# Scalings of the softmax on three engines, unit orders tried at build time, and norms spread by transposes

## The chip, the cores and the metric

The kernel runs on one core of one Trainium2 chip. Its engines are TensorE (PE, matrix products, with PEld for the loading of the stationary operand), VectorE (DVE), ScalarE (ACT), GpSimd (POOL) and SyncE (SP), whose queue issues every DMA here. The metric is device time of one execution in microseconds (us). All data is float32; the products run in three passes over operands that are split into a high and a low part.

## The reference, cut to what matters

512 tokens of 1024 features pass through four stages. Each begins with an RMS norm over the 1024 features of a token.

```
layer A : x + (rglru(conv(h@w_in)) * silu(gate)) @ w_out          h = rmsnorm(x, g)
layer B : x + (swa(q, k, v) * silu(gate)) @ w_out                 16 heads of 64, window 128, sinks
block 2 : x + (sig(ga)*(gqa@w_a) + sig(gb)*(nbr@w_b)) @ w_out      8 heads of each kind
MLP     : x + relu(rmsnorm(x)@w_up)**2 @ w_down, then a last rmsnorm

softmax of a head, with its sink:  p = exp(s - m) / (sum(exp(s - m)) + exp(sink - m))
rmsnorm:                           y = x * rsqrt(mean(x*x) + eps) * g
```

## The kernel before

Activations are kept transposed, features on partitions and the 512 tokens along the free axis. Each product of a 128x128 weight tile with 512 tokens is three matmuls (high x high, high x low, low x high). A weight column block of 128 outputs (a "unit", 512 KB for 1024 inputs) is brought in by a DMA from SP's queue, copied to its high part (ACT, DVE or POOL, lines 322 and 331) and subtracted to its low part (DVE, line 346).

The order of the work is not written out. Each piece is a generator that yields operations, and a planner (`Sched`) runs when the kernel is built: it keeps a clock per engine with a price for each operation, takes among the operations that could start soonest the one of the best priority, and emits it. What it emits is the order of each engine's queue on the chip, where every engine then works in order. So a change of a price, a priority or a limit moves instructions on all engines.

Three parts of it matter here.

- **Norms** (`rstd_chain`). Four matmuls with a column of ones (line 396, 128x1) sum the squares of the 512 tokens, one column of 128 tokens each; POOL raises the mean to the power -0.5 (line 386), which gives `col`, 128 partitions by 4 columns. What the later stages need is the same numbers along the free axis on all partitions (`nrm.bc`). For that DVE multiplies the identity by `col` (128x512, line 346), one product with a matrix of ones spreads it (`ps<-fb,ones`, two hardware passes), and ACT copies it out of PSUM (line 322). The norms a, b, m and f stand ahead of layer A, layer B, block 2 and the MLP.
- **Attention units** (`attn_unit`). One unit is 4 heads of one block of 128 queries (in the neighborhood attention one head of all 512). It scales the mask (layer B only, line 374), multiplies q and k (matmuls with 256 or 384 columns), takes maximum and sum of mask and scores on DVE (line 972, its own code), exponentiates on ACT, multiplies by the reciprocal of the sum (line 374, four times), transposes on TensorE (line 420), splits, and multiplies by v. Both scalings are `PMUL`, which has POOL alone. At most `MAXU` = 4 units are under way at a time. Layer B has 16 units, block 2 eight of the first kind and eight of the second.
- **Work beside the units.** While units run, TensorE is filled with the projections of the same stage (`main`, in a fixed order). In layer B the last of these is `b_w_out`, whose first products take features 0 to 5 of 8 and whose later ones need features 6 and 7, which come from the last four units.

PSUM has 8 banks; a unit holds one for each pair of score products until DVE has read them.

Of the kernel before, what the change touches and what calls it, by code (L numbers as in the profile page):

```python
# [15 lines left out]
P = 128  # L16
# [14 lines left out]
MAXU = 4  # L31
# [4 lines left out]
AVOID = 600.0  # L36
# [37 lines left out]
class Op:  # L74
# [3 lines left out]
    def __init__(self, opts, reads, writes):  # L78
# [3 lines left out]
        self.ready = None  # L82


class Task:
    def __init__(self, gen, prio):
        self.gen = gen
        self.prio = prio
        self.op = None


class Sched:
# [3 lines left out]
    def __init__(self):  # L96
# [20 lines left out]
    def spawn(self, gen, prio=3):  # L117
        t = Task(gen, prio if callable(prio) else (lambda: prio))
        self.tasks.append(t)
        return t  # L120

# [26 lines left out]
    def run(self):  # L148
        while self.tasks:
# [12 lines left out]
            for t in self.tasks:  # L162
                if isinstance(t.op, Op):
                    best = None
                    for o, rdy in zip(t.op.opts, t.op.ready):
                        c = self.clock[o[0]]
                        s = max(c, rdy)
                        f = s + o[1] + (AVOID if o[0] == "POOL" and len(t.op.opts) > 1 else 0.0)
# [23 lines left out]
            emit()  # L192
# [55 lines left out]
def kernel(ctx: ExitStack, tc: tile.TileContext, io: dict, out: bass.AP):  # L248
    nc = tc.nc
    S = Sched()  # L250
# [56 lines left out]
    def A(o, i, fn, scale=None, bias=None, accum=None, also=None):  # L307
# [30 lines left out]
        return Op(opts, rd, wr)  # L338
# [304 lines left out]
    def rstd_chain(nrm):  # L643
# [1039 lines left out]
    layer_a()  # L1683
    layer_b()
    block2()
    mlp()

    def main():
        for fn in jobs:
            yield from fn()  # L1690
# [9 lines left out]
    with tc.manual_schedule():  # L1700
# [15 lines left out]
        S.run()  # L1716
# [117 lines left out]

# [15 lines left out]
```

## Time and profile before

| what | us |
|---|---|
| median of 3 runs | 1137.48 (1136.98 to 1137.63) |
| the profiled execution | 1139.5 |
| its span, first to last instruction | 1137.7 |
| TensorE busy | 1119.6 |
| VectorE / ScalarE / GpSimd busy | 758.7 / 384.1 / 306.6 |

The profiled execution lies 2.0 us above the median, 1.8 us of its time is outside the span. A busy TensorE is not a TensorE at its peak: matmuls are pipelined, so the busy time of one overlaps that of the next, and what a matmul costs is the step from its start to the next start.

### The profile page before, as it was taken

How to read it: one execution, taken by the hardware profiler on the slowest of the kernel's cores; microseconds unless marked ns; L12 is line 12 of the kernel's file. 1: busy time of each engine (PE TensorE's matmuls, PEld its weight loads, DVE VectorE, ACT ScalarE, POOL GpSimd, SP SyncE). 2: the span in 40 equal slices, each digit the busy share in tenths (PEclk: the TensorE clock that was granted, in tenths of full speed). 3: DMA queues.
4: the chain of work that ended last, by engine and by line, in shares of the span. 5: the costliest groups of instructions: out<-in, count | busy, mean ns of one | idle time of the engine just before them, and what ended most of it. 6: DMA issues, size and time to landing. Idle time of an engine off the chain costs nothing.

```text
span 1137.7 us, 14747 instructions
## 1 busy us (share of the span) xinstructions
PE 1119.6 (98%) x5316; PEld 931.7 (82%) x5316; DVE 758.7 (67%) x1344; ACT 384.1 (34%) x781; POOL 306.6 (27%) x404
## 2 busy tenths in 40 slices
PE   8999999999999899999999999999999999999997
PEld 6788888888888688788888888888888888888887
DVE  7999998775777886568666565876554225556332
ACT  5457761234566631156444251111111111111001
POOL 1222333135586532032322224312110003113100
PEclk9999999999999899999999999999999999999998
DMA  7333445108133330820463645523233322223001
GB/s 290 87 117 107 145 141 193 56 1 257 40 96 95 134 102 12 238 102 29 134 191 111 176 133 174 185 75 111 79 117 118 112 74 89 78 93 111 1 1 74
DMA packets 46793, 127.42 MB, mean 112 GB/s; under 512 B 6272, under 2 KB 7936, under 8 KB 46720
## 3 DMA queue, kind: packets, MB, share of 16 engines
q1 hardware_dynamic: 46720, 126.47, 35.0%
q8 instruction: 42, 0.69, 0.2%
q14 instruction: 31, 0.25, 0.1%
HBM read 106.53 MB, written 2.10 MB: 95 GB/s over the span
## 4 chain that ended last, share of the span: by engine, by line
PE 93%; DVE 2%; issue 2%; DMA 1%; ACT 1%; POOL 1%; SPq 0%; POOLq 0%; DVEq 0%
PE ps L396 90%; PE ps L420 3%; DVE fb L360 1%; DMA fb<-in_mk 1%; POOL fb L374 0%; DMA fb<-in_x 0%; DVE rb L346 0%; SPq L426 0%; ACT rb L322 0%; DVE fb L346 0%; ACT fb L322 0%; DMA rb<-rb 0%; DVE fb L972 0%; DVE fb L1632 0%; POOLq L1846 0%
## 5 line engine op out<-in xcount | busy, mean ns | idle before, releaser
L396 PE MATMUL ps<-rb 128*128 128x512 f32 (+2 forms) x4856 | 1087.1, 383 | 5.1 <-DMA rb<-rb 1.6
L396 PEld LDWEIGHTS ps<-rb 128*128 128x128 f32 x4856 | 878.0, 188 | 177.6 <-issue 3.0
L331 POOL TENSOR_SCALAR rb<-fb 128x1024 fp32r<-128x1024 f32 (+5 forms) x163 | 175.5, 1087 | 564.2 <-PE ps L396 407.4
L346 DVE TENSOR_TENSOR rb<-fb,rb 128x1024 fp32r<-128x1024 f32 (+5 forms) x305 | 289.0, 972 | 40.9 <-ACT rb L322 37.1
L322 ACT ACTIVATE rb<-fb 128x512 fp32r<-128x512 f32 (+4 forms) x131 | 96.9, 745 | 307.0 <-DVE fb L360 155.4
L346 DVE TENSOR_TENSOR fb<-ps,fb 128x512 f32<-128x512 f32 (+3 forms) x142 | 83.6, 590 | 156.7 <-PE ps L396 141.0
L374 POOL TENSOR_SCALAR fb<-fb,sm 128x256 f32<-128x256 f32 (+2 forms) x128 | 74.9, 603 | 125.3 <-DVE sm L389 97.1
L346 DVE TENSOR_TENSOR fb<-fb 128x512 f32<-128x512 f32 (+1 forms) x120 | 88.9, 747 | 23.3 <-ACT rb L322 21.1
L360 DVE SCALAR_TENSOR_TENSOR fb<-ps,fb 128x512 f32<-128x512 f32 x56 | 38.5, 688 | 58.4 <-PE ps L396 58.3
L346 DVE TENSOR_TENSOR rb<-ps,rb 128x512 fp32r<-128x512 f32 (+2 forms) x86 | 52.3, 612 | 37.5 <-ACT rb L322 35.5
L322 ACT ACTIVATE fb<-fb 128x512 f32<-128x512 f32 (+1 forms) x66 | 39.4, 612 | 102.6 <-DVE fb L346 83.7
L322 ACT ACTIVATE rb<-ps 128x512 fp32r<-128x512 f32 (+2 forms) x86 | 46.0, 538 | 82.1 <-PE ps L420 73.8
L322 ACT ACTIVATE fb<-fb,sm 128x256 f32<-128x256 f32 (+2 forms) x128 | 65.2, 512 | 21.2 <-DVE sm L368 16.1
L322 ACT ACTIVATE rb<-fb,vec 128x512 fp32r<-128x512 f32 x41 | 28.4, 719 | 101.1 <-DVE fb L346 98.9
L322 ACT ACTIVATE fb<-ps 64x256 f32<-64x256 f32 (+2 forms) x68 | 30.1, 442 | 82.5 <-PE ps L396 72.4
L420 PE MATMUL ps<-ident,fb 128*128 128x128 f32 x328 | 52.3, 276 | 5.4 <-POOL fb L374 4.5
L420 PEld LDWEIGHTS ps<-ident,fb 128*128 128x128 f32 x328 | 41.3, 142 | 17.2 <-POOL fb L374 6.2
L972 DVE CUSTOM_DVE_ANT_0 fb<-ps,fb 128x256 f32<-128x256 f32 (+1 forms) x64 | 29.4, 486 | 10.8 <-DMA fb<-in_mk 5.2
L972 DVE CUSTOM_DVE_ANT_0 fb<-ps,fb,sm_qs 128x256 f32<-128x256 f32 (+1 forms) x64 | 27.0, 443 | 7.3 <-PE ps L396 4.9
L374 POOL TENSOR_SCALAR fb<-fb,sm_qt 128x256 f32<-128x256 f32 (+1 forms) x64 | 30.6, 498 | 2.2 <-DMA fb<-in_mk 2.2
L360 DVE SCALAR_TENSOR_TENSOR rb<-fb,vec,rb 128x512 fp32r<-128x512 f32 x41 | 30.5, 763 | 0.6 <-ACT rb L322 0.4
L360 DVE SCALAR_TENSOR_TENSOR fb<-fb,vec 128x512 f32<-128x512 f32 x36 | 30.2, 856 | 0.0
(84 smaller groups left out, 327.0 us busy)
## 6 DMA issues: line engine op xcount, KB each, us to landing
rb<-rb SPq DMA_DIRECT2D x128, 128.0 KB, 2.5
fb<-in_w_down SPq DMA_DIRECT2D x32, 512.0 KB, 3.7
fb<-in_w_in SPq DMA_DIRECT2D x31, 512.0 KB, 4.2
fb<-in_w_up SPq DMA_DIRECT2D x29, 512.0 KB, 3.5
fb<-in_a_w_in SPq DMA_DIRECT2D x22, 512.0 KB, 3.7
fb<-in_b_w_in SPq DMA_DIRECT2D x16, 512.0 KB, 4.7
fb<-in_mb SPq DMA_DIRECT2D x8, 640.0 KB, 5.9
fb<-in_a_w_out SPq DMA_DIRECT2D x8, 512.0 KB, 3.8
```

What stands on the lines that cost most here:

```text
L322: opts = [("ACT", dur, lambda: nc.scalar.activation(out=o, in_=i, func=fn, **kw), TABLES.get(fn))]
L331: lambda: nc.gpsimd.tensor_scalar(out=o, in0=i, scalar1=1.0, scalar2=1.0, op0=ALU.mult, op1=ALU.mult), None,
L346: lambda: nc.vector.tensor_tensor(out=o, in0=a, in1=b, op=op), None,
L360: lambda: nc.vector.scalar_tensor_tensor(out=o, in0=a, scalar=s, in1=b, op0=op0, op1=op1), None,
L374: lambda: nc.gpsimd.tensor_scalar(out=o, in0=a, scalar1=s, scalar2=1.0, op0=ALU.mult, op1=ALU.mult), None,
L396: nc.tensor.matmul(out=o, lhsT=l, rhs=r, start=st, stop=sp)
L420: nc.tensor.transpose(o, i, ident)
L972: nc.vector.tensor_tensor_reduce(out=pt[h], in0=PS[:, b, o0:o0 + nk], in1=m, scale=sc, scalar=-3.0e38, op0=ALU.add, op1=ALU.max, accum_out ...
```

## The change

`PMUL` gets three choices (POOL, ACT with 800 ns added to its end in the comparison, DVE with 1200 ns), and the penalty for POOL in the operations that could run elsewhere moves from the planner into the operation. `MAXU` goes from 4 to 6. Each task of the planner gets a random number between 0 and 1 added to its priority, drawn from a seed per stage; before the kernel is built, the planner runs through each of the four stages with 8 seeds without emitting anything, and the seed whose TensorE clock is lowest at the end of the stage is kept (seed 0 adds nothing). The numbers drawn here are 0, 1, 5 and 0 for layer A, layer B, block 2 and the MLP. In `rstd_chain` the product with the identity and the product with ones go; in their place TensorE transposes each column of `col`, repeated 128 times by its access pattern.

```diff
-MAXU = 4
+MAXU = 6
-AVOID = 600.0
+JITTER = 1.0
+ORDERS = 8
...
+    def draw(self, t):
+        t.noise = JITTER * self.rng.random() if self.rng else 0.0
+
+    def next_part(self):
+        self.part += 1
+        if self.part == len(self.seeds):
+            if self.trial:
+                raise Enough()
+            return
+        self.rng = random.Random(self.seeds[self.part]) if self.seeds[self.part] else None
+        for t in self.tasks:
+            self.draw(t)
...
-                        f = s + o[1] + (AVOID if o[0] == "POOL" and len(t.op.opts) > 1 else 0.0)
+                        f = s + o[1] + t.op.late.get(o[0], 0.0)
...
-                        score = t.prio() - max(age, 0.0) / AGE
+                        score = t.prio() + t.noise - max(age, 0.0) / AGE
...
     def PMUL(o, a, s):
-        return Op([(
-            "POOL", 262.0 + 0.832 * _free(o),
-            lambda: nc.gpsimd.tensor_scalar(
-                out=o, in0=a, scalar1=s, scalar2=1.0, op0=ALU.mult, op1=ALU.mult
-            ), None,
-        )], [a, s], [o])
+        n = _free(o)
+        return Op([
+            ("POOL", 262.0 + 0.832 * n, lambda: nc.gpsimd.tensor_scalar(
+                out=o, in0=a, scalar1=s, scalar2=1.0, op0=ALU.mult, op1=ALU.mult), None),
+            ("ACT", 286.0 + 0.833 * n, lambda: nc.scalar.activation(out=o, in_=a, func=AF.Copy, scale=s), None),
+            ("DVE", 220.0 + 0.524 * n, lambda: nc.vector.tensor_scalar(
+                out=o, in0=a, scalar1=s, scalar2=None, op0=ALU.mult), None),
+        ], [a, s], [o], {"ACT": 800.0, "DVE": 1200.0})
...
-        dg = yield from fa.get()
-        yield TT(
-            f_(dg).rearrange("p (b t) -> p b t", b=4),
-            ident.unsqueeze(1).to_broadcast([P, 4, P]),
-            col.unsqueeze(2).to_broadcast([P, 4, P]),
-            ALU.mult,
-        )
         b = yield from pa.get()
-        yield MMS([(p_(b), ones, f_(dg), True, True, 858.0)])
-        fa.free(dg)
+        yield TRS([(PS[:, b, j * P:(j + 1) * P], col[:, j:j + 1].to_broadcast([P, P])) for j in range(4)])
         yield A(f_(bc), p_(b), AF.Copy)
...
+def _orders(arrays):
+    arrays = {name[3:]: v for name, v in arrays.items()}
+    best = ()
+    for _ in range(4):
+        times = []
+        for seed in range(ORDERS):
+            try:
+                times.append((_trial(arrays, best + (seed,)), seed))
+            except AssertionError:
+                pass
+        best += (min(times)[1],)
+    return best
```

What moves, engine by engine, at three places. Of the 192 scalings that stood on POOL, 27 are now on ACT (16 of masks, 11 of exponentials) and 10 on DVE (5 and 5).

**Place 1: TensorE's queue at norm a, early in layer A.** `ones,fb` are the sums of squares, `fb,ones` the product with ones, `ident,col_a` the transposes. Before:

```order
L396 MATMUL ps<-rb 128x512 x69
L396 MATMUL ps<-ones,fb 128x1 x4
L396 MATMUL ps<-rb 128x512 x15
L396 MATMUL ps<-fb,ones 128x512
L396 MATMUL ps<-rb 128x512 x915
```

and after the change:

```order
L426 MATMUL ps<-rb 128x512 x69
L426 MATMUL ps<-ones,fb 128x1 x4
L426 MATMUL ps<-rb 128x512 x12
L450 MATMUL ps<-ident,col_a 128x128 x4
L426 MATMUL ps<-rb 128x512 x918
```

The spreading stands three matmuls earlier and is four transposes. Norms m and f move the same way; at norm b the transposes stand where the product stood.

**Place 2: TensorE's queue at the end of layer B's attention.** The first row is the last group of score products (256 columns); `ident,fb` are the transposes of probabilities, four or eight in a row, which wait for the scalings; the 512-column rows are projections and products with v. Before (followed by eight transposes, 8 matmuls, four transposes and 183 matmuls):

```order
L396 MATMUL ps<-rb 128x256 x4
L396 MATMUL ps<-rb 128x512 x3
L420 MATMUL ps<-ident,fb 128x128 x4
L396 MATMUL ps<-rb 128x512 x16
L420 MATMUL ps<-ident,fb 128x128 x4
L396 MATMUL ps<-rb 128x512 x10
L420 MATMUL ps<-ident,fb 128x128 x8
L396 MATMUL ps<-rb 128x512 x3
L420 MATMUL ps<-ident,fb 128x128 x4
L396 MATMUL ps<-rb 128x512 x10
L420 MATMUL ps<-ident,fb 128x128 x4
L396 MATMUL ps<-rb 128x512 x5
```

and after the change (followed by 8 matmuls, four transposes, 5 matmuls, four transposes and 166 matmuls):

```order
L426 MATMUL ps<-rb 128x256 x4
L450 MATMUL ps<-ident,fb 128x128 x8
L426 MATMUL ps<-rb 128x512 x35
L450 MATMUL ps<-ident,fb 128x128 x4
L426 MATMUL ps<-rb 128x512 x15
L450 MATMUL ps<-ident,fb 128x128 x4
L426 MATMUL ps<-rb 128x512 x31
L450 MATMUL ps<-ident,fb 128x128 x4
L426 MATMUL ps<-rb 128x512 x9
L450 MATMUL ps<-ident,fb 128x128 x4
L426 MATMUL ps<-rb 128x512 x8
L450 MATMUL ps<-ident,fb 128x128 x4
```

Between the last scores and the last transposes stand 55 matmuls before and 111 after. Behind the last transposes the first matmul that waits for features 6 and 7 is the 49th before and the 32nd after.

**Place 3: SP's queue where block 2's first mask (`in_mk`, 128x1536) is fetched.** `rb<-rb` are moves of q and k parts between partitions, `in_w_in` weight units. Before:

```order
L426 DMA rb<-rb 64x512 x4
L426 DMA fb<-in_w_in 128x1024
L426 DMA rb<-rb 64x512 x4
L426 DMA fb<-in_w_in 128x1024
L426 DMA fb<-in_mk 128x1536
L426 DMA rb<-rb 64x512 x4
L426 DMA fb<-in_w_in 128x1024
L426 DMA fb<-in_mk 128x1536
```

and after the change:

```order
L456 DMA rb<-rb 64x512 x4
L456 DMA fb<-in_w_in 128x1024
L456 DMA rb<-rb 64x512 x4
L456 DMA fb<-in_mk 128x1536
L456 DMA fb<-in_w_in 128x1024
L456 DMA rb<-rb 64x512 x4
L456 DMA fb<-in_mk 128x1536
```

The mask is issued ahead of one weight unit that it followed. TensorE's queue at the same place, from the first score products of block 2 on, before:

```order
L396 MATMUL ps<-rb 128x384 x4
L396 MATMUL ps<-rb 128x512 x3
L396 MATMUL ps<-rb 128x256 x8
L396 MATMUL ps<-rb 128x384 x4
L396 MATMUL ps<-rb 128x256 x4
L396 MATMUL ps<-rb 128x512 x15
L396 MATMUL ps<-rb 128x384 x4
```

and after the change:

```order
L426 MATMUL ps<-rb 128x384 x2
L426 MATMUL ps<-rb 128x256 x4
L426 MATMUL ps<-rb 128x384 x2
L426 MATMUL ps<-rb 128x256 x4
L426 MATMUL ps<-rb 128x512 x3
L426 MATMUL ps<-rb 128x384 x2
L426 MATMUL ps<-rb 128x256 x4
L426 MATMUL ps<-rb 128x384 x2
L426 MATMUL ps<-rb 128x512 x6
L426 MATMUL ps<-rb 128x384 x2
```

Seven groups of score products (two matmuls of 384 columns, or four of 256, fill a bank) now stand with 3 matmuls of 512 columns among them where 3 stood too, and the eighth comes after 6 more instead of 15.

## Rows read from the trace of the kernel before

**Rows 1.** The page: its head, and busy time (share of the span) and instructions.

```profile
span 1137.7 us, 14747 instructions
PE 1119.6 (98%) x5316; PEld 931.7 (82%) x5316; DVE 758.7 (67%) x1344; ACT 384.1 (34%) x781; POOL 306.6 (27%) x404
```

**Rows 2.** TensorE's waits: total us, times, longest us.

```profile
PE ps L420 <- POOL fb L374: 4.5, 4, 1.6
PE ps L396 <- DMA rb<-rb: 1.6, 2, 1.4
PE ps L396 <- DVE sm L972: 1.5, 1, 1.5
```

**Rows 3.** Stretches: length, busy us (instructions) by engine, clock, DMA share, GB/s.

```profile
380.00:400.00 20.00, 15.47 (x66) 11.56 (x66) 15.62 (x40) 14.06 (x43) 11.81 (x19) 0.83 0.53 184
...
460.00:480.00 20.00, 20.00 (x97) 16.88 (x95) 8.19 (x12) 3.19 (x3) 1.06 (x1) 1.00 0.99 266
...
389.00:395.00 6.00, 5.95 (x18) 4.79 (x19) 3.93 (x9) 2.39 (x7) 4.72 (x10) 0.54 0.73 246
```

**Rows 4.** The chain that ended last: start us, us, what.

```profile
251.23 0.44 PE ps L420 x4
...
688.09 413.86 PE ps L396 x1830
...
1104.34 6.47 PE ps L396 x54
```

**Rows 5.** Timeline at norms a and b: start us, us, engine, line, count.

```profile
25.25 3.71 PE L396 MATMUL ps<-rb 128*128 128x512 f32 x15
...
26.46 1.03 POOL L386 TENSOR_TENSOR col_a<-sm,half 128x4 f32<-128x4 f32 x1 [24.49 <-DVE sm L368]
...
28.90 1.13 PE L396 MATMUL ps<-fb,ones 128*128 128x512 f32 x2
...
30.06 0.60 ACT L322 ACTIVATE fb<-ps 128x512 f32<-128x512 f32 x1 [9.73 <-PE ps L396]
...
244.53 1.02 PE L396 MATMUL ps<-fb,ones 128*128 128x512 f32 x2
...
249.51 1.02 PE L396 MATMUL ps<-fb,hones 128*128 128x512 f32 x2
```

**Rows 6.** The chain at layer A's first gate products.

```profile
50.83 1.94 DMA rb<-rb
```

**Rows 7.** Timeline at the end of layer B's attention.

```profile
373.44 2.10 PE L396 MATMUL ps<-rb 128*128 128x512 f32 x10
...
379.85 2.57 PE L396 MATMUL ps<-rb 128*128 128x512 f32 x10
...
382.96 6.04 POOL L374 TENSOR_SCALAR fb<-fb,sm 128x256 f32<-128x256 f32 x8 [6.73 <-DVE sm L389]
...
389.18 1.63 PE L396 MATMUL ps<-rb 128*128 128x512 f32 x3
...
389.79 3.98 POOL L374 TENSOR_SCALAR fb<-fb,sm 128x256 f32<-128x256 f32 x8 [0.79 <-DVE sm L389]
...
399.54 0.60 PE L420 MATMUL ps<-ident,fb 128*128 128x128 f32 x4
...
407.03 3.56 DVE L346 TENSOR_TENSOR rb<-fb,rb 128x512 fp32r<-128x512 f32 x4
```

**Rows 8.** The chain at block 2's first scores.

```profile
472.60 8.01 DMA fb<-in_mk
...
481.71 3.33 PE ps L396 x16
```

**Rows 9.** Groups by line and form: busy us, mean ns, idle before.

```profile
L1571 DVE TENSOR_SCALAR fb<-fb,vec 128x256 f32<-128x256 f32 x4 | 1.4, 354 | 0.1
L331 POOL TENSOR_SCALAR rb<-fb 128x1024 fp32r<-128x1024 f32 x103 | 129.2, 1260 | 492.5 <-PE ps L396 359.4 <-DMA fb<-in_w_in 27.4 <-DVE rb L346 23.5
```

**Rows 10.** DMA issues: count, KB each, median us to landing.

```profile
fb<-in_w_in SPq DMA_DIRECT2D x31, 512.0 KB, 4.2
```

More of the change, by code (lines that the diff above doesn't have):

```diff
@@ L1 @@
+import random
 from contextlib import ExitStack
@@ L74, with __init__ @@
 class Op:
-    def __init__(self, opts, reads, writes):
+    def __init__(self, opts, reads, writes, late=None):
         self.opts = opts
@@ L82, in __init__ @@
         self.ready = None
+        self.late = late or {}
 class Task:
@@ L89, in __init__ @@
         self.op = None
+        self.noise = 0.0
+class Enough(Exception):
+    pass
 class Sched:
-    def __init__(self):
+    def __init__(self, seeds=(0,), trial=False):
+        self.seeds = seeds
+        self.trial = trial
+        self.part = 0
+        self.rng = random.Random(seeds[0]) if seeds[0] else None
         self.clock = dict.fromkeys(("PE", "ACT", "DVE", "POOL", "SP"), 0.0)
@@ L118, in spawn @@
         t = Task(gen, prio if callable(prio) else (lambda: prio))
+        self.draw(t)
         self.tasks.append(t)
         return t
+    def draw(self, t):
[8 more added lines that the diff above has]
+        for t in self.tasks:
+            self.draw(t)
     def _ready(self, op, eng):
@@ L191, in run @@
                 self.table = tab[0]
-            emit()
+            if not self.trial:
+                emit()
             if eng == "SP":
@@ L247, with kernel @@
 @with_exitstack
-def kernel(ctx: ExitStack, tc: tile.TileContext, io: dict, out: bass.AP):
+def kernel(ctx: ExitStack, tc: tile.TileContext, io: dict, out: bass.AP, seeds=(0,), trial=False):
     nc = tc.nc
-    S = Sched()
+    S = Sched(seeds, trial)
     const = ctx.enter_context(tc.tile_pool(name="const", bufs=1))
@@ L337, in A @@
             ))
-        return Op(opts, rd, wr)
+        return Op(opts, rd, wr, {"POOL": 600.0})
     def TT(o, a, b, op, eng="DVE"):
@@ L1681, in mlp @@
         add([wsl("w_down", n, a, e) for n in last for a, e in segs], fn)
[L1683 to L1686, printed above, removed]
+    ends = []
+    for stage in (layer_a, layer_b, block2, mlp):
+        stage()
+        ends.append(len(jobs) + 3)
     def main():
-        for fn in jobs:
+        for i, fn in enumerate(jobs):
+            if i in ends:
+                S.next_part()
             yield from fn()
@@ L1715 @@
         S.spawn(main(), 5)
-        S.run()
+        try:
+            S.run()
+        except Enough:
+            return S.clock["PE"]
     return ra.peak, fa.peak, pa.peak, max(S.clock.values())
@@ L1832, in _layout, with _trial @@
     return d
+def _trial(arrays, seeds):
+    import concourse.bacc as bacc
+    nc = bacc.Bacc("TRN2", target_bir_lowering=False, num_devices=1)
+    io = {
+        name: nc.dram_tensor(f"in_{name}", v.shape, mybir.dt.from_np(v.dtype), kind="ExternalInput").ap()
+        for name, v in arrays.items()
+    }
+    o = nc.dram_tensor("out_y", (T, D), F32, kind="ExternalOutput").ap()
+    with tile.TileContext(nc) as tc:
+        r = kernel(tc, io, o, seeds, True)
+    return r[3] if isinstance(r, tuple) else r
+def _orders(arrays):
[4 more added lines that the diff above has]
+        for seed in range(ORDERS):
+            try:
+                times.append((_trial(arrays, best + (seed,)), seed))
+            except AssertionError:
+                pass
+        best += (min(times)[1],)
+    return best
 def kernel(**inputs):
@@ L1846 @@
     with tile.TileContext(nc) as tc:
-        kernel(tc, io, o)
+        kernel(tc, io, o, _orders(arrays))
     res = run_bass_kernel_spmd(nc, [arrays], core_ids=[0]).results[0]["out_y"]
```

## The prediction

> **What bounds the kernel now.** Read the shares of busy time first: TensorE is busy for 1119.6 of 1137.7 us, no other engine for more than 67% [rows 1]. So a change pays only where TensorE stands still, runs at the lower clock, or does something that it need not do. The step of a matmul comes from a long undisturbed piece of the chain: 1830 matmuls of 512 columns in 413.86 us are 0.226 us each; 54 of 256 columns in 6.47 us are 0.12 us each; four transposes take 0.44 us [rows 4]. The reader is to see that in that piece, the whole MLP up to 1102 us, there is nothing to win.
>
> Then TensorE's own waits: 4.5 us on GpSimd's scalings, 1.6 us on moves between partitions, 1.5 us on VectorE's maximum [rows 2]. Third, the stretches: from 380 to 400 us TensorE is busy for 15.47 of 20 us and the granted clock is 0.83, and from 389 to 395 us 0.54 [rows 3], that is near 1.2 instead of 2.4 GHz, right after the wait. So the largest loss is one place, the end of layer B's attention, and it is paid twice.
>
> **What each part costs or gives back.**
>
> Term 1, norm a and the start. In the kernel before, the power ends at 26.46 + 1.03 = 27.49 us, the product with ones begins at 28.90 and ACT's copy at 30.06, 1.16 us after the product's start [rows 5]. After the change the transposes stand 12 instead of 15 matmuls behind the sums: 25.25 + 12 x 0.226 = 27.96 us, later than the power's end, so they can start there. They take 0.44 us instead of the 0.9 of the product, and if the rest of the distance to the copy stays (0.26 us), the copy begins at 28.7 instead of 30.06, 1.4 us sooner. From there to the first gate products VectorE sets the pace, with the same work in nearly the same order, and the last step is the 1.94 us move that TensorE waits for at 50.83 us [rows 6]. The data is 1.4 us sooner; TensorE, whose wait there is 1.6 us [rows 2], arrives some 0.5 us sooner. So the whole 1.4 us comes through. Bounds: 0.5 (TensorE's own saving alone) to 1.6 + 0.5 = 2.1.
>
> Term 2, norms b, m and f. What a product with ones costs is read at norm b: from its start at 244.53 to the next special product at 249.51 are 4.98 us, in which 18 matmuls of 0.226 stand, so 0.91 us is its own [rows 5]. Four transposes are 0.44 us [rows 4], 0.47 less, three times 1.4 us. All of it is TensorE's time where nothing is waited for. No row shows a transpose whose stationary operand repeats one column; its bounds are the known transposes (gain 1.4) and the product that it replaces (gain 0); it is nearer to the known transposes, which differ only in where the operand is read. The identity's product on VectorE, which goes, was hidden at these three.
>
> Term 3, the end of layer B's attention. Before: the ten matmuls from 379.85 us are done at 379.85 + 10 x 0.226 = 382.1, and the next ordinary matmul begins at 389.18 [rows 7]. Between them stand only eight transposes, 0.9 us. So 7.1 - 0.9 = 6.2 us are waited, GpSimd's 4.5 of them by the wait view. Then the low clock: 5.4 us lie at half speed (1 - 0.54 of 6 us, doubled, is 5.5), in which up to half is lost, 2.7 us, less what transposes and waits in it would have taken anyway; I count 2.4. Together 8.6 us.
>
> How much of that stays? The last scores before lie 3 matmuls into the row at 373.44, at 374.1 to 374.6 us [rows 7]. Measured from 374.6, the scalings of the last four units end at about 386 and 389.0 (eight in 6.04 us from 382.96) and at 391.8 and 393.8 (eight in 3.98 us from 389.79): 11, 14.4, 17.2 and 19.2 us behind the last scores. After the change 35, 50, 81, 90, 98, 106 and 111 matmuls stand between the last scores and the seven groups of transposes of the last four units; with the transposes themselves that is 8.8, 12.6, 20, 22.5, 25, 27 and 28.5 us. If the scalings end as before, counted from the last scores, only the first unit is late, by 11 - 8.8 = 2 us, and less if its eight do not share GpSimd with the busiest VectorE stretch, since the same eight cost 6.04 us there and 3.98 us later; I take 0.9. Behind the last transposes 31 matmuls stand before `b_w_out` needs features 6 and 7: 0.44 + 31 x 0.226 = 7.4 us. Before, from the last transposes at 399.54 to the first of the low parts, 407.03 + 0.89, were 8.4 us, hidden under 48 matmuls. So about 1 us comes back there. I keep 2.0 of the 8.6 us and gain 6.6. Bounds: 8.6 gained (no wait) to none (the same wait elsewhere). A wait of some 1.5 us had no drop of the clock behind it at 480 us (clock 1.00 in its stretch [rows 3]), so with the wait the 2.4 us should go too.
>
> Term 4, block 2's first mask. Before: issued at 472.60, landed 8.01 us later, and TensorE, out of PSUM banks, resumed at 481.71 [rows 8] after 1.5 us [rows 2]. After: the mask stands ahead of a 512 KB weight unit. At the 266 GB/s of that stretch [rows 3] the unit is 2.0 us of transfer, so the mask is landed 2.0 us sooner or better. But TensorE also runs out of banks sooner: 8 matmuls of 384, 12 of 256 and 18 of 512 columns stand between the first scores and the eighth bank before, 8, 12 and 9 after; at 0.226 us for 512, 0.12 for 256 and 0.17, between the two, for 384 columns that is 6.9 and 4.8 us, 2 us sooner. By transfer time alone the two cancel. Bounds: the wait gone (gain 1.5) to a mask that lands no sooner, so a wait of 3.5 (loss 2.0). I take a gain of 0.7: the weight unit also competed with the mask while both were under way, so the 2.0 us are the least that its going ahead gives.
>
> Term 5, new waits. Both attention stages have another order, with six units under way. In the old order TensorE waited nowhere else in them, so there is nothing to gain and something to lose; the nearest row is the wait of 1.5 us at the start of an attention stage [rows 2]; I take half of one, 0.7, with bounds 0 and 4.5 (three such).
>
> The scalings that leave GpSimd are worth nothing by themselves: 37 of 192, and at place 2 the last units' scalings still stand on GpSimd.
>
> Sum: 1.4 + 1.4 + 6.6 + 0.7 - 0.7 = 9.4 us. Against the profiled execution that is 1139.5 - 9.4 = 1130.1 (span 1128.3); that execution lies 2.0 above the median of the runs, so for the median 1137.5 - 9.4 = **1128.1 us**.
>
> **A rule against it.** A scaling of 256 columns on VectorE takes 0.354 us where such an instruction stands now [rows 9], and eight on GpSimd take 3.98 or 6.04 us, by what VectorE does beside them [rows 7]. The Trainium skill (SBUF — State Buffer, "Who interferes with whom") says that VectorE and GpSimd share one pair of ports, that a `tensor_scalar` in a two-port mode takes the pair for its whole length, and that the other engine then fully blocks. The two times of the eight scalings agree with such a coupling, though no row shows a two-port instruction doing it. By that rule the ten scalings on VectorE would hold GpSimd for 10 x 0.354 = 3.5 us, and if all of that came to TensorE the sum would be 5.9 us, 1131.6. That is a rival below, with a small chance, since the ten stand in four places and none of them among the last units of layer B.
>
> **The rivals.**
>
> A: the wait only shrinks by half. The last units' chain is as long as before and `b_w_out` catches up with it. For it: 31 matmuls against 8.4 us; the first unit has 8.8 us against 11. Against it: 20 us and more for the other three. With 5.3 us kept, 3.3 more than taken, 1131.4.
>
> B: the waits only move. Same total, so that only the four norms' 4 x 0.47 = 1.9 us remain: 1135.6. For it: the amount of softmax work is the same and VectorE is busy for 15.62 us of the 20 [rows 3]. Against it: 56 more matmuls, 12.7 us, between the last scores and the last transposes.
>
> C: slower. Six units hold more of the 38 buffers that weights land in too, so weight units are issued later and TensorE waits for them: 4.2 us to land [rows 10] and 1.26 us for the high part [rows 9] are 5.5 us for each unit that is issued only when it is needed. One such eats half the gain (1133.6); from two on, with the clock falling behind a wait as long as the one at 382 us, 9.4 - 11.0 - 2.4 = -4.0, so 1141.5. Against it: in SP's queue no weight unit stands behind more moves than before at the places shown.
>
> D: GpSimd blocked by VectorE, 1131.6.
>
> **How the numbers follow.** The forecast has 0.60, A 0.20, D 0.04, B 0.08, C 0.08. The forecast's own range goes from all waits gone (1.4 + 1.4 + 8.6 + 1.5 = 12.9, 1124.6) to 1130.5. The range 1124 to 1133.5 takes in A and D and leaves out B, C and the ends of the forecast, not quite 2 in 10. About 0.2%, 2.3 us, is what this kernel's measurement can tell from no change: forecast, A and D are faster, 0.84; B is the same, 0.08; C is slower, 0.08.
>
> **What would show it.** In the profile after: no wait of transposes on scalings above 2 us in all, a granted clock of 1.00 in every stretch between 20 and 1110 us (term 3 right; a stretch below 0.9 near 370 to 395 us is A or B). ACT's copy of norm a near 28.7 us and the first gate products about 1.4 us sooner (term 1). Four transposes at each norm in 0.44 us (term 2). TensorE's wait on the maximum at block 2's start under 1.5 us (term 4). Waits on weight high parts or low parts of more than 3 us would make the prediction wrong on the side of C.

## The result and the profile after

The changed kernel takes 1129.09 us (median of 5 runs, 1128.61 to 1129.27) against 1137.63 us in the runs beside it (1136.98 to 1138.4): a ratio of 0.9921, 95% interval 0.991 to 0.9932, or 8.5 us less. The forecast was 1128.1 us. The profiled executions differ by more, 1139.5 and 1129.1 us, because the one of before lies 2 us above its median.

The head of the page and the busy times, to be read beside [rows 1]:

```profile
span 1127.3 us, 14746 instructions
PE 1115.4 (99%) x5324; PEld 931.0 (83%) x5324; DVE 762.4 (68%) x1349; ACT 404.0 (36%) x823; POOL 269.2 (24%) x353
```

TensorE has eight more instructions (four transposes in place of two hardware passes, at four norms) and stands still less. Its waits after, in total us, times and longest, answer to [rows 2]:

```profile
PE ps L426 <- ACT rb L350: 2.5, 2, 1.5
...
PE ps L450 <- DVE fb L1593: 0.9, 1, 0.9
PE ps L450 <- DVE sm L388: 0.3, 1, 0.3
PE ps L426 <- DVE rb L374: 0.2, 1, 0.2
```

All three waits of [rows 2] are gone: transposes on GpSimd's scalings, moves between partitions, block 2's maximum. The first row holds one wait at the start (1.5) and one of 1.0 us at the end of layer B. The stretches of [rows 3], with the same columns, after:

```profile
380.00:400.00 20.00, 20.00 (x99) 16.54 (x98) 15.53 (x32) 9.77 (x26) 11.88 (x16) 1.00 0.76 257
460.00:480.00 20.00, 20.00 (x108) 17.52 (x108) 15.56 (x55) 3.44 (x11) 1.05 (x1) 1.00 0.69 209
389.00:395.00 6.00, 6.00 (x34) 5.00 (x33) 4.55 (x8) 3.38 (x9) 3.38 (x5) 1.00 0.71 211
```

From 380 to 400 us TensorE now does 99 matmuls instead of 66, at a granted clock of 1.00 instead of 0.83. TensorE's timeline there, after (answers to [rows 7]; start us, us, engine, line, count, and in brackets the idle time and what ended it):

```profile
373.84 0.60 PE L450 MATMUL ps<-ident,fb 128*128 128x128 f32 x4
...
393.95 0.60 PE L450 MATMUL ps<-ident,fb 128*128 128x128 f32 x4
394.31 7.32 PE L426 MATMUL ps<-rb 128*128 128x512 f32 x31
402.64 0.50 PE L426 MATMUL ps<-rb 128*128 128x512 f32 x1 [1.01 <-ACT rb L350]
403.37 4.85 PE L426 MATMUL ps<-rb 128*128 128x512 f32 x20 [0.22 <-DVE rb L374]
```

No row from 373.84 to 393.95, those left out here included, has a bracket: TensorE does not wait there. What is left stands behind the 31 matmuls that cover features 6 and 7: from 394.31 to 403.37 are 9.06 us for 32 matmuls of 0.226 us, so 1.8 us are lost.

To compare kernels whose orders differ, the table gives the time on TensorE between the first square sums of one norm (the matmuls of one column) and those of the next, from one profiled execution each; the ratio to before comes from many runs.

| kernel | layer A | layer B | block 2 | MLP | ratio to before (95%) |
|---|---|---|---|---|---|
| before | 215.05 | 202.01 | 335.43 | 334.65 | 1 |
| after | 212.69 | 196.33 | 333.07 | 334.22 | 0.9921 (0.991 to 0.9932) |
| e1, norms alone | 212.73 | 202.53 | 338.77 | 334.21 | 1.0033 (1.0023 to 1.0043) |
| e2, six units alone | 215.03 | 203.03 | 338.51 | 334.65 | 1.0082 (1.0062 to 1.0102) |
| e3, three engines alone | 216.66 | 201.29 | 335.15 | 334.65 | 1.0019 (1.0009 to 1.0028) |
| e4, after, GpSimd alone, seeds of after | 212.87 | 200.07 | 333.05 | 334.22 | 0.9962 (0.9947 to 0.9977) |
| e5, norms, order of before | 214.41 | 200.21 | 333.09 | 334.22 | 0.9984 (0.9974 to 0.9995) |
| e6, after, GpSimd alone, same order | 212.67 | 205.20 | 333.35 | 334.22 | 0.9975 (0.9965 to 0.9984) |
| e7, after, no choice of orders | 212.52 | 199.54 | 340.92 | 334.22 | 1.0002 (0.9992 to 1.0012) |
| e8, choice of orders alone | 215.07 | 199.53 | 333.53 | 334.64 | 0.9982 (0.9972 to 0.9991) |
| e9, after, four units, own seeds | 212.56 | 203.05 | 333.01 | 334.22 | 0.9976 (0.9964 to 0.9988) |
| e10, after, GpSimd alone, own seeds | 212.52 | 198.91 | 333.25 | 334.22 | 0.9957 (0.994 to 0.9973) |
| e11, after, five columns open | 212.61 | 196.57 | 333.50 | 334.22 | 0.9909 (0.9894 to 0.9924) |
| e12, after, 40 orders | 212.57 | 195.79 | 333.07 | 334.22 | 0.991 (0.9896 to 0.9925) |

A profiled execution can lie 2 to 3.5 us off its kernel's median (e5: 1134.3 against 1136.47; e2: 1143.92 against 1147.45), so a difference of a stage is trusted here where several kernels repeat it or where a row names the wait.

### The profile page after: what moved, and what is told of

The parts are those of the page before. It is cut to its first block, busy times and chain, and to the rows that moved or that the text cites. A ratio compares the mean times of both kernels' runs of the same rounds, so it can differ in the third digit from the quotient of the medians.

```text
span 1127.3 us, 14746 instructions
## 1 busy us (share of the span) xinstructions
PE 1115.4 (99%) x5324; PEld 931.0 (83%) x5324; DVE 762.4 (68%) x1349; ACT 404.0 (36%) x823; POOL 269.2 (24%) x353
## 4 chain that ended last, share of the span: by engine, by line
PE 93%; DVE 2%; issue 1%; DMA 1%; SPq 1%; POOL 1%; ACT 1%; POOLq 0%; DVEq 0%; ACTq 0%
PE ps L426 90%; PE ps L450 3%; SPq L456 1%; DMA fb<-in_mk 1%; DMA fb<-in_a_w_in 0%; DVE rb L374 0%; ACT rb L350 0%; DVE fb L374 0%; POOL fb L402 0%; DVE fb L994 0%; POOL col_b L416 0%; DVE fb L405 0%; DVE rb L388 0%; ACT fb L350 0%; DVE fb L388 0%
## 5 line engine op out<-in xcount | busy, mean ns | idle before, releaser
L374 DVE TENSOR_TENSOR rb<-fb,rb 128x1024 fp32r<-128x1024 f32 (+5 forms) x305 | 297.3, 995 | 69.4 <-ACT rb L350 58.0
L359 POOL TENSOR_SCALAR rb<-fb 128x1024 fp32r<-128x1024 f32 (+4 forms) x149 | 156.9, 1062 | 611.6 <-PE ps L426 479.9
L350 ACT ACTIVATE rb<-fb 128x512 fp32r<-128x512 f32 (+4 forms) x149 | 109.2, 741 | 357.1 <-DVE fb L388 164.2
L402 POOL TENSOR_SCALAR fb<-fb,sm 128x256 f32<-128x256 f32 (+2 forms) x112 | 64.8, 595 | 118.4 <-DVE sm L419 76.9
L450 PE MATMUL ps<-ident,fb 128*128 128x128 f32 x328 | 49.8, 272 | 1.2 <-DVE fb L1593 0.9
L994 DVE CUSTOM_DVE_ANT_0 fb<-ps,fb 128x256 f32<-128x256 f32 (+1 forms) x64 | 28.8, 487 | 11.4 <-PE ps L426 9.5
L350 ACT ACTIVATION_READ_ACCUMULATOR fb<-fb,sm 128x1 f32 x128 | 24.1, 189 | 0.0
```

The lines of the kernel that those rows point to most:

```text
L350: opts = [("ACT", dur, lambda: nc.scalar.activation(out=o, in_=i, func=fn, **kw), TABLES.get(fn))]
L359: lambda: nc.gpsimd.tensor_scalar(out=o, in0=i, scalar1=1.0, scalar2=1.0, op0=ALU.mult, op1=ALU.mult), None,
L374: lambda: nc.vector.tensor_tensor(out=o, in0=a, in1=b, op=op), None,
L402: ("POOL", 262.0 + 0.832 * n, lambda: nc.gpsimd.tensor_scalar(out=o, in0=a, scalar1=s, scalar2=1.0, op0=ALU.mult, op1=ALU.mult), None),
L450: nc.tensor.transpose(o, i, ident)
L994: nc.vector.tensor_tensor_reduce(out=pt[h], in0=PS[:, b, o0:o0 + nk], in1=m, scale=sc, scalar=-3.0e38, op0=ALU.add, op1=ALU.max, accum_out ...
```

## The experiments

**First, each edit alone.** If each pays for itself, they add up to the change.

e1 takes the norms only; the planner then writes its order anew.

```diff
-        yield MMS([(p_(b), ones, f_(dg), True, True, 858.0)])
+        yield TRS([(PS[:, b, j * P:(j + 1) * P], col[:, j:j + 1].to_broadcast([P, P])) for j in range(4)])
```

> The kernel before with the norms by transposes and nothing else of the change. Theory D (distance): what is lost at the end of layer B's attention depends only on how far the last seven groups of transposes stand behind the last scores, however that order came about. The written order moves here too: the groups stand 9.5 us or more of matmuls behind the last scores (7.4 before), and 30 matmuls (48 before) between the last transposes and the first use of features 6 and 7. By the scalings' ends of before (11, 14.4, 17.2 and 19.2 us) the largest shortfall is 1.5 us instead of 8.6 us with the low clock, so 7.1 and the norms' 2.8 are gained: 1137.6 - 9.9 = 1127.7 us. Rival S (each edit pays for itself): only the norms' 2.8 us, 1134.8 us, and the wait and the low clock near 385 us stay.

Measured: 1141.21 us, ratio 1.0033. Both theories fail. Layer A gains as in the changed kernel, but the end of layer B loses as much as before in another way. Block 2 is 3.3 us longer in this trace, although its wait on the first mask is gone, by a loss at a place where the kernel before lost nothing. TensorE in e1 at both places:

```profile
380.42 0.33 PE L420 MATMUL ps<-ident,fb 128*128 128x128 f32 x1
381.12 0.68 PE L420 MATMUL ps<-ident,fb 128*128 128x128 f32 x3 [0.37 <-POOL fb L374]
383.52 0.51 PE L396 MATMUL ps<-rb 128*128 128x512 f32 x1 [1.72 <-DVE rb L326]
384.45 2.07 PE L396 MATMUL ps<-rb 128*128 128x512 f32 x4 [0.43 <-DVE rb L346]
...
703.73 1.83 PE L396 MATMUL ps<-rb 128*128 128x512 f32 x8
707.83 0.49 PE L396 MATMUL ps<-rb 128*128 128x512 f32 x1 [2.27 <-DVE rb L326]
```

The wait on scalings is down to 0.37 us, as Theory D had it. But the output product behind it now catches up with the features that the units finish, and waits for their split (a cast on line 326, a subtraction on line 346). In block 2 the same happens at its last units. The clock falls behind both, and a third time behind a wait of 1.57 us for a feature at 408 us:

```profile
380.00:390.00 10.00, 7.49 (x26) 5.28 (x25) 7.60 (x20) 6.31 (x25) 6.01 (x13) 0.83 0.78 269
700.00:710.00 10.00, 7.15 (x33) 5.17 (x32) 6.26 (x11) 2.63 (x7) 8.14 (x15) 0.92 0.90 293
```

e2 takes six units only.

```diff
-MAXU = 4
+MAXU = 6
```

> The kernel before with up to six instead of four units under way, nothing else. Theory D: the first of the last seven groups stands 12.9 us behind the last scores, so no transpose waits for a scaling for more than 0.5 us; but only 23 matmuls (5.2 us) and four transposes stand before features 6 and 7 are needed, whose chain took 8.4 us, so 2.8 us are waited there. Gain 8.6 - 2.8 = 5.8 us: 1131.8 us. Rival S with six units as the cause: the whole 6.6 us of term 3, 1131.0 us, with no new wait behind the last transposes. Rival S with the three engines as the cause: 1137.6 us.

Measured: 1147.45 us, ratio 1.0082, the slowest of all. The places in its trace:

```profile
336.22 1.19 PE L396 MATMUL ps<-rb 128*128 128x512 f32 x4 [2.16 <-DVE rb L346]
...
408.64 0.50 PE L396 MATMUL ps<-rb 128*128 128x512 f32 x1 [2.38 <-ACT rb L322]
...
710.53 0.49 PE L396 MATMUL ps<-rb 128*128 128x512 f32 x1 [1.91 <-DVE rb L326]
```

No transpose waits for a scaling, and the wait for feature 6 has about the size expected (2.4 against 2.8 us). Waits that no theory had, at 336 to 338 us (2.16 and 1.02 us) and at 710 us, make it slow, with the clock behind the waits at 408 and 710 us (0.83 in the 10 us from 410 and from 710 us); behind those at 336 us it stayed at 1.00. The other three runs are 3.4 to 4.1 us longer than this profiled one, for a reason that no trace here shows.

e3 takes the three engines only.

```diff
-        return Op([(
-            "POOL", 262.0 + 0.832 * _free(o),
...
+            ("ACT", 286.0 + 0.833 * n, lambda: nc.scalar.activation(out=o, in_=a, func=AF.Copy, scale=s), None),
...
+        ], [a, s], [o], {"ACT": 800.0, "DVE": 1200.0})
```

> The kernel before with the scalings on three engines, nothing else. Theory D: the groups stand at 8.1 us and more behind the last scores, the largest shortfall against the scalings' old ends is 3.0 us, less as far as scalings of the last units leave GpSimd; 42 matmuls cover features 6 and 7. Gain 8.6 - 3.0 = 5.6 us: 1132.0 us, and with scalings that end sooner down to 1129. Rival S with the three engines as the cause of term 3: 6.6 us, 1131.0, with scalings of the last units on ScalarE or VectorE and the groups' waits gone for that reason. Rival that six units are the cause: 1137.6.

Measured: 1139.67 us, ratio 1.0019. Transposes still wait for GpSimd's scalings, 5.1 us in all, the longest here:

```profile
389.50 0.69 PE L423 MATMUL ps<-ident,fb 128*128 128x128 f32 x2 [2.48 <-POOL fb L375]
```

So three engines do not remove that wait by themselves. It is not what makes e3 slower in this trace either: layer B is 0.7 and block 2 is 0.3 us shorter than before. Layer A is 1.6 us longer, because the clock fell (0.83 from 50 to 60 us) behind the same wait of 1.38 us for moves that the kernel before, e2 and e5 have with the clock at 1.00 there. Whether e3's other runs share that is not shown. Alone, with the order written anew, each of the three edits is slower.

**Second, the parts at a fixed order.** e5 leaves the order of before and replaces only what is emitted for the norms (the planner still plans product and multiplication); e6 leaves the order of after and puts the 37 scalings back on GpSimd.

```diff
 e5
-        yield MMS([(p_(b), ones, f_(dg), True, True, 858.0)])
+        plan = MMS([(p_(b), ones, f_(dg), True, True, 858.0)])
+        real = TRS([(PS[:, b, j * P:(j + 1) * P], col[:, j:j + 1].to_broadcast([P, P])) for j in range(4)])
+        plan.opts = [(o[0], o[1], real.opts[0][2]) + tuple(o[3:]) for o in plan.opts]
+        yield plan
 e6
+        g = lambda: nc.gpsimd.tensor_scalar(out=o, in0=a, scalar1=s, scalar2=1.0, op0=ALU.mult, op1=ALU.mult)
-            ("ACT", 286.0 + 0.833 * n, lambda: nc.scalar.activation(out=o, in_=a, func=AF.Copy, scale=s), None),
+            ("ACT", 286.0 + 0.833 * n, g, None),
```

> The kernel before with the norms by transposes, but with every instruction left where it stands before: the planner still plans the product and its multiplication. Theory O (order): the norms pay 2 us up to the first gate products (as the traces of the changed kernel and of the first experiment show) and about 0.5 us each at b, m and f, and nothing else moves, so the wait and the low clock near 385 us stay: 1137.5 - 3.4 = 1134.1 us. The prediction's terms 1 and 2 give 2.8: 1134.7. Rival: the transposes gain only where the order moves too: 1137.5 us.

Measured: ratio 0.9984 (0.6 to 3.0 us less by the interval), 1136.47 us. The norms alone, with nothing moved, are a small gain; the expected 3.4 us lie outside the interval, the prediction's 2.8 within. Norm a in e5, in the timeline:

```profile
28.81 0.60 PE L420 MATMUL ps<-ident,col_a 128*128 128x128 f32 x4
...
29.45 0.60 ACT L322 ACTIVATE fb<-ps 128x512 f32<-128x512 f32 x1 [9.13 <-PE ps L420]
...
40.00 10.74 SPq L426 DMA_DIRECT2D rb<-rb  x9
...
52.19 2.11 PE L396 MATMUL ps<-rb 128*128 128x512 f32 x8 [1.38 <-DMA rb<-rb]
```

The copy starts 0.61 us sooner than in [rows 5], TensorE and the moves are both that much sooner, and the wait of 1.38 us stays. Its wait of transposes on scalings stays too, 4.3 us in all.

> The changed kernel with every instruction in its place, and only the engine of the 37 scalings that left GpSimd put back to GpSimd. The prediction said that the scalings that leave are worth nothing by themselves: 1129.1 us. Rival (GpSimd's relief is what pays): GpSimd is busy for 9.74 of 10 us from 350 to 360 us in the changed kernel, and each scaling put back adds about 0.6 us; eight of them in the last units of an attention make 4.8 us, and with a low clock behind the wait the time is 1134 to 1136 us.

Measured: 1135.11 us, ratio 0.9975, against 0.9921: about 6 us lost, the rival's size, though the place is another. GpSimd and TensorE in e6 near 325 us:

```profile
325.37 7.29 POOL L401 TENSOR_SCALAR fb<-fb,sm_qt 128x128 f32<-128x128 f32 x16
...
333.18 0.33 PE L449 MATMUL ps<-ident,fb 128*128 128x128 f32 x1 [2.18 <-POOL fb L401]
```

and GpSimd in the changed kernel, with ScalarE taking the rest:

```profile
324.78 3.79 POOL L402 TENSOR_SCALAR fb<-fb,sm_qt 128x128 f32<-128x128 f32 x9
```

These are the scalings of the mask, sixteen at once when it lands. With nine on GpSimd they take 3.79 us, with sixteen 7.29, and maximum, reciprocal, the next scalings and the transposes come after them. Not all of layer B's 205.20 us need be theirs: in this trace the first mask landed 7.8 us behind its issue (5.8 in the changed kernel, whose DMAs are issued in the same order), and TensorE waits 0.6 and 0.8 us at 274 and 277 us for maxima behind it. The 6 us come from ten runs, of which the profiled one is the longest, 2.6 us above the median.

**Third, the choice among orders.** e7 is the changed kernel with seed 0 at each stage, e8 the kernel before with the choice alone, e4 the changed kernel with the scalings on GpSimd and the seeds chosen for three engines, e10 the same with the seeds that its own trials choose, e9 the changed kernel with four units and its own seeds.

```diff
 e7
-        tile_blocks_kernel(tc, io, o, _orders(arrays))
+        tile_blocks_kernel(tc, io, o, (0, 0, 0, 0))
```

> The changed kernel with seed 0 at every stage, that is without a choice among orders. Theory O: the gain beyond the norms comes from choosing an order. In this one only 7 matmuls stand between the last transposes and the first use of features 6 and 7 (31 in the changed kernel), whose chain takes 8.4 us: 6.4 us waited against 1.7, and up to 2.4 for a low clock: 1133.8 to 1136.2 us. Theory E (norms, six units and three engines gain when together, whatever the order): 1129.1 us.

Measured: 1137.75 us, ratio 1.0002. With seed 0 everywhere, nothing of the 8.5 us is left, not even the norms' share. TensorE in e7 at the two places:

```profile
398.14 2.16 PE L426 MATMUL ps<-rb 128*128 128x512 f32 x7
403.54 0.49 PE L426 MATMUL ps<-rb 128*128 128x512 f32 x1 [3.24 <-ACT rb L350]
...
700.25 1.25 PE L450 MATMUL ps<-ident,fb 128*128 128x128 f32 x10
...
705.52 6.87 PE L426 MATMUL ps<-rb 128*128 128x512 f32 x15 [2.13 <-DVE rb L354]
```

The first was expected from the count of seven matmuls. The second, with a clock of 0.76 from 700 to 710 us, costs block 2 7.9 us (340.92 against 333.07), at a place that no expectation named.

> The kernel before with the trial orders alone: norms by products, four units, all scalings on GpSimd; seeds 0, 5, 5 and 0, which its own trials choose. Theory O: some of the 8.6 us at the end of layer B's attention comes back by the choice alone. By the scalings' ends of before the largest shortfall in this order is 3.7 us and 43 matmuls cover features 6 and 7: gain 4.9 us, 1132.6 us. Theory E: 1137.5 us or, as with the other edits made alone, slower.

Measured: 1135.33 us, ratio 0.9982; a gain, though half of what was expected. Layer B is 2.5 us shorter than before.

> The changed kernel with every scaling on GpSimd again; norms, six units and the four chosen seeds stay. Theory D: the first groups stand 7.4 and 8.5 us behind the last scores (shortfall 3.6 us, at first), the later ones are covered, and 21 matmuls before features 6 and 7 leave 3.2 us. Since the first wait pushes the rest back, the two don't add: 3.6 us lost against 1.7 measured in the changed kernel, 1131.0 us, or up to 2.4 more if the clock falls. Rival S (three engines as the cause): the 6.2 us of wait and the low clock come back, 1136 us. Rival that the scalings' engine means nothing: 1129.1 us.

Measured: 1132.93 us, ratio 0.9962, within Theory D's 1131.0 to 1133.4 us. Of its two places one is right: no transpose waits for a scaling, so the shortfall of the first groups did not come, and the loss is at feature 6 (3.92 us of wait where the count of matmuls had 3.2), with the clock at 0.83 from 400 to 410 us:

```profile
405.88 0.54 PE L424 MATMUL ps<-rb 128*128 128x512 f32 x1 [3.92 <-ACT rb L350]
```

> The changed kernel with all scalings on GpSimd and the seeds that its own trials choose then (0, 5, 1, 0). Theory O: an order chosen for it hides GpSimd's scalings; the groups stand short by 2.2 us at most and 48 matmuls cover features 6 and 7: 1129.6 us, layer B 197 us between its norms. Theory G (ScalarE's share of the scalings is itself needed, as the sixth experiment's 205.2 us in layer B would have it): a wait of transposes on scalings of 2 us or more stays, layer B takes 200 us, 1133 us.

Measured: 1132.39 us, ratio 0.9957. Theory G is nearer to the time but has not the cause: no transpose waits for a scaling. TensorE waits for the low part of transposed probabilities, which VectorE subtracts from PSUM (`rb<-ps,rb`) behind the transposes of the first row.

```profile
379.06 1.03 PE L448 MATMUL ps<-ident,fb 128*128 128x128 f32 x8
...
384.39 1.84 PE L424 MATMUL ps<-rb 128*128 128x512 f32 x4 [3.25 <-DVE rb L374]
```

> The changed kernel with four units under way and the seeds that its own trials choose then (0, 3, 1, 0). Theory O (the choice of an order is the cause, whatever it chooses among): about the gain of the changed kernel, with the 3.5 us at most that its first three groups stand short at the end of layer B's attention (7.5 us behind the last scores against scalings that ended at 11): 1129 to 1132.5 us. Theory U (six units give the choice its room; with four, the best order still ends the attention in a wait): layer B takes 200 us or more between its norms (196.3 in the changed kernel, 199.5 with the trials alone), 1133 us or more.

Measured: 1135.36 us, ratio 0.9976, layer B 203.05 us. Theory U holds: with four units the chosen order still ends the attention in waits, with the clock at 0.77 from 380 to 390 us.

```profile
384.07 1.11 PE L450 MATMUL ps<-ident,fb 128*128 128x128 f32 x7 [2.01 <-POOL fb L402]
386.67 0.79 PE L426 MATMUL ps<-rb 128*128 128x512 f32 x1 [1.49 <-DVE rb L354]
```

So six units, the slowest edit alone, are worth 0.0055 of 1137.6, some 6 us, with one chosen order on either side.

**Fourth, what is left.** e11 opens the output product with five column blocks, e12 chooses among 40 orders.

```diff
 e11
-        gemm_open("b_w_out", [0, 1, 2, 3], 6, KD, y1, ev, 1)
-        for j in range(4, KD):
+        gemm_open("b_w_out", [0, 1, 2, 3, 4], 6, KD, y1, ev, 1)
+        for j in range(5, KD):
 e12
-        tile_blocks_kernel(tc, io, o, _orders(arrays))
+        tile_blocks_kernel(tc, io, o, (26, 10, 25, 0))
```

> The changed kernel with the same seeds, but layer B's output product opens with five groups of columns instead of four, so that 54 instead of 31 matmuls stand between the last transposes and the first use of features 6 and 7. If the 1.8 us lost there in the changed kernel is only missing cover, it goes: layer B 194.6 us between its norms, ratio to before 0.9906, 1127.4 us. Rival: the fifth bank of PSUM is missed by the last units' products with the values, or the chain behind the last transposes takes longer for other reasons: 1129 us or more.

Measured: 1127.22 us, ratio 0.9909. The wait near 402 us is gone, and another has come near 276 us, in the same execution:

```profile
276.18 2.18 PE L426 MATMUL ps<-rb 128*128 128x256 f32 x10 [2.23 <-DVE sm L994]
...
394.60 17.75 PE L426 MATMUL ps<-rb 128*128 128x512 f32 x77
```

That wait hangs on the mask, which landed 7.9 us behind its issue here and 5.8 in the changed kernel, with the same DMAs ahead of it in the queue. So the edit does what it should, and this execution hides it: layer B is 196.57 us in this trace, as in the changed kernel.

> The changed kernel with the best of 40 instead of 8 trial orders at each stage (seeds 26, 10, 25 and 0). If the choice among orders goes by what the chip then does, more of them give a shorter time: 1127 us or less. Rival: the planner's durations miss the waits that remain (the groups stand 9 us behind the last scores, 28 matmuls before features 6 and 7: 1.6 to 2 us lost at the end of layer B's attention), so that more trials give nothing: 1129 us within 1.5.

Measured: 1127.65 us, ratio 0.991. The loss at feature 6 is there as the rival said (1.9 us beyond the usual steps of the matmuls, with waits of 0.54 and 0.69 us in it), and the time is within the rival's 1129 give or take 1.5. Both e11 and e12 have intervals that reach across that of the changed kernel (0.991 to 0.9932), so neither is shown to beat it; both beat the kernel before.

## Why the prediction was right, step by step

**What it had right.** It read the new order and counted, place by place, which matmuls cover which chain. The largest term came out so: layer B is 5.7 us shorter, of which some 0.4 belong to its norm (as in the MLP), so 5.3 against 6.6 less 0.7 for new waits. The scalings' wait and the low clock went; what was to stay at `b_w_out` was put at about 1 us and is 1.8. The wait allowed at the first unit's transposes (0.9 us) did not come. A slip there cost nothing: 386.0 less 374.6 are 11.4 us, not 11.

**What was luck.** By stage the sum had 1.4, 6.4, 1.2 and 0.5 us; the two traces differ by 2.4, 5.7, 2.4 and 0.4, less 0.4 at the start, which makes 10.4 in place of 9.4. The medians moved by 8.5. That the forecast lies 1 us from the measured median is better than its terms are, since their errors have both signs.

**Term 1, size and reason off.** Layer A is 2.36 us shorter instead of 1.4. The copy starts at 29.18 us, 0.88 sooner than in [rows 5] and not 1.36, since the sums themselves begin 0.44 us later. The step that has the data 1.4 us sooner and TensorE 0.5 failed. In e5 both are sooner alike, 0.6 us, and the wait stays. What removed it is the order of VectorE's work. In the changed kernel

```profile
29.18 0.60 ACT L350 ACTIVATE fb<-ps 128x512 f32<-128x512 f32 x1 [8.75 <-PE ps L450]
...
38.13 11.08 SPq L456 DMA_DIRECT2D rb<-rb  x9
```

the nine moves start 2.5 us sooner than before (40.62) and 1.9 sooner than in e5 (40.00). e1, which has the new norms and neither six units nor other seeds, has that too (38.03). The moves start as ScalarE's copy of their tile ends, and the copy waits for VectorE: it starts at 37.47 us, in e5 at 39.34. In e5 a subtraction of 0.95 us (128x768, at 37.04) stands in VectorE's queue ahead of what the copy waits for, in the changed kernel behind it (38.09).

**Term 2, right.** The MLP's stage, which holds norm f and no other part of the change, takes 334.21 or 334.22 us in all ten kernels with transposes and 334.64 or 334.65 in the four without: 0.43 us, predicted 0.47. A transpose whose stationary operand repeats one column costs no more than another: both step by 0.108 to 0.110 us in the changed kernel.

**Term 4, right sign, not shown to be the change's.** The wait on block 2's maximum is gone, 1.9 us instead of 0.7. But in e5, with the order of before, it is gone as well. VectorE's first maximum there:

```profile
475.84 0.43 DVE L977 CUSTOM_DVE_ANT_0 fb<-ps,fb 128x256 f32<-128x256 f32 x1 [3.53 <-DMA fb<-in_mk]
```

Its mask, issued at 469.73, landed 6.0 us later, in the profile of before 8.01 [rows 8], with all DMAs issued in the same order. Block 2 is 333.09 us in e5 and 333.07 in the changed kernel. So the order of before has no such wait when the mask lands sooner, and the 1.9 us can be those of one late transfer. In the other thirteen traces, most with other orders, block 2's first mask landed in 4.2 to 6.3 us; how often the kernel before meets 8 us, no run here shows.

**Term 5.** New losses beyond the usual steps came, 0.3 us at 274.7 and at 365.7 us and 0.5 us at 304.1, 1.1 in all, predicted 0.7. Of the three only 0.3 us, at 304.1, counts as a wait in the view above.

**The step that failed.** "The scalings that leave GpSimd are worth nothing by themselves." In e6 they are worth 6 us. The prediction took the last units' scalings, which but for one (ScalarE, 381.66 us) did stay on GpSimd, and not the mask's, of which sixteen come at once. In the kernel before they also take some 7 us on GpSimd, under cover; in the new order, as e6's waits show, they have less. The time came out all the same, because the sum was read from the new order, which has the scalings where they went.

**The rivals.** A's place was the right one for what remains, with 1.8 instead of 5.3 us. B did not happen here, but in e1 it did: the same loss behind another wait. C's late weights were not seen: behind the changed kernel's first 8 us no wait of TensorE is on a weight. But its sign was: e1 and e2 are slower, with waits mostly on the units' chains, e3 for a reason that its trace leaves open. D's mechanism is there, its price is not (below). A's 5.3 us kept and the upper end of 1130.5 for the forecast stand in the prediction without a working.

**What it did not ask.** It took the order as given and predicted its effect, which is why the time came out. It does not say what each edit gives, and the edits do not add up: alone they are +3.8, +9.3 and +2.2 us by their ratios, and all of them without a choice 0.2. Taken from the changed kernel one by one, the choice is worth 9.2 us (e7), six units 6.3 (e9), three engines 4.1 (e10, with its own seeds); the norms were not taken out of it. Each figure compares one order with one other, and orders alone differ by as much (e4 to e10), so what a part is worth over many orders is not shown. That a single edit's loss lies in the order written with it is shown for the norms (0.9984 in the old order, 1.0033 in the new one), and by e7 for all three together; for six units or three engines alone it was not tried.

## What to carry to other kernels

Where a planner writes the order, an edit of a price or a limit is an edit of the whole order: test it at a fixed order to know the part's worth, and with the order chosen anew to know what it is worth in use. Count the matmuls between a producer and its use, for every chain at a stage's end, not only for the one that waits now; when one wait is covered, the next chain of the same units is behind it. Before a wait on a transfer is booked as a gain, look whether another execution with the same order has it.

## What the runs showed of the hardware

**VectorE and GpSimd take turns when both scale the mask.** They do so side by side in the changed kernel (timeline of both):

```profile
271.64 2.23 DVE L405 TENSOR_SCALAR fb<-fb,sm_qt 128x256 f32<-128x256 f32 x5 [3.14 <-DMA fb<-in_mk]
271.71 2.78 POOL L402 TENSOR_SCALAR fb<-fb,sm_qt 128x256 f32<-128x256 f32 x6 [4.29 <-DMA fb<-in_mk]
```

and the groups by form (busy us, mean ns) give VectorE's scaling beside GpSimd and alone:

```profile
L405 DVE TENSOR_SCALAR fb<-fb,sm_qt 128x256 f32<-128x256 f32 x4 | 1.8, 514 | 3.1 <-DMA fb<-in_mk 3.1
...
L405 DVE TENSOR_SCALAR fb<-fb,sm 128x256 f32<-128x256 f32 x1 | 0.4, 353 | 0.0
```

Eleven scalings, eight of 256 columns and three of 128, are done in 2.85 us (271.64 to 274.49). VectorE's with 256 columns take 354 ns for the first and 561 to 576 for the next three, instead of 353. GpSimd's four take 631 and then 502 to 505 ns; where VectorE is idle throughout, the median of 14 such is 476 ns. The ends alternate: each of GpSimd's four ends 0.33 to 0.35 us behind a scaling of VectorE's, and VectorE's next one 0.14 to 0.15 us behind that. The recorded times overlap, so a turn is shorter than a record, and the waiting for it lies inside the record. The Trainium skill (SBUF — State Buffer, "Who interferes with whom") has the other engine fully blocked for the instruction when VectorE runs a `tensor_scalar` in a two-port mode; the rows agree with such turns, but no row tells which mode these ran in. The price is not that of the prediction's D: beside five scalings on VectorE, GpSimd's six take 2.88 us instead of 2.64, where 5 x 0.354 would be 1.8 us more. The rest of the cost falls on VectorE.

**VectorE's subtractions between SBUF tiles hold GpSimd's scalings up far more.** Of the scalings of 256 columns on GpSimd in the changed kernel's trace, 25 began with VectorE idle (470 to 484 ns) and 51 beside a VectorE instruction that reads PSUM (472 to 483 ns, but for one of 1171). Ten began during a subtraction with both operands in SBUF (`rb<-fb,rb`); they take 637 to 1529 ns, and eight of them end 0.345 to 0.347 us behind the subtraction. One such is the first of the three scalings here:

```profile
285.94 1.23 DVE L374 TENSOR_TENSOR rb<-fb,rb 128x1024 fp32r<-128x1024 f32 x1
286.07 2.35 POOL L402 TENSOR_SCALAR fb<-fb,sm 128x256 f32<-128x256 f32 x3
```

This is also in the prediction's eight scalings of 6.04 us [rows 7]: the first began during a subtraction and took 1.02 us. In e6 one of 1.51 us, begun during a subtraction of 1.22 us, lies in the wait at 333 to 335 us.

**A transfer's landing scatters by as much as a term of the sum.** The first mask of layer B, with the same DMAs ahead of it in the queue, landed in 5.8 us in the changed kernel, 7.9 in e11 and 7.8 in e6; 2.1 us are more than any term of the sum but the third.

**The same wait is followed by half clock in one execution and not in another.** In its trace the changed kernel runs at half clock near its start, the kernel before does not:

```profile
8.00:10.00 2.00, 2.00 (x5) 1.20 (x6) 1.97 (x4) 2.00 (x4) 0.00 (x0) 0.68 1.06 405
10.00:12.00 2.00, 2.00 (x6) 1.57 (x5) 2.00 (x5) 2.00 (x5) 0.00 (x0) 0.50 1.06 419
```

Ahead of it stands one wait of 1.49 us; in the kernel before two, 1.07 and 0.29 us, with a few matmuls between and a clock of 1.00. This is not the kernel's own: e11, with the same matmuls in the same order there, waited 1.21 us and kept a clock of 1.00, and e5 kept it behind 1.50 us. Behind the wait of 1.38 us for moves in layer A, e3 fell and the kernel before, e2 and e5 did not. At the start it costs little: the first sums come 0.44 us later than in the trace of before and 0.56 later than in e11's.
